# Products with the values alternated between a pair's two heads, the output projection's first chunk amid the pairs, and rows 128 to 255 turned in score banks

## The chip, the core and the metric

The kernel runs on one core of a Trainium2 chip. TensorE (PE in the rows; PEld is its weight load) multiplies, VectorE (DVE) and ScalarE (ACT) do the elementwise work and empty PSUM, GpSimd (POOL) and SyncE (SP) issue most of the transfers. PSUM has eight banks of 128 partitions by 512 float32 values here. The metric is the device time of one execution in microseconds (us), the median of several. Less is better.

## What is computed

Two residual layers over 512 tokens of width 1024. Layer 0 mixes tokens by causal pooling, layer 1 by dilated sliding-window attention; after each mixer comes a SwiGLU feed-forward with 2816 hidden units, and a last rmsnorm ends it. The change touches only layer 1's mixer:

```python
def attn_mixer(h, w_qkv, w_out):
    qkv = jnp.einsum('bsd,de->bse', h, w_qkv).reshape(B, S, 3, N_HEADS, HEAD_DIM)
    q = rope(qkv[:, :, 0]) * HEAD_DIM ** -0.5
    k, v = rope(qkv[:, :, 1]), qkv[:, :, 2]
    ...
    for (window, dilation), n_g in zip(((128, 1), (512, 4), (2048, 16)), (6, 5, 5)):
        o_g, lse_g = dilated_window_attention(q[:, :, sl], k[:, :, sl], v[:, :, sl], window, dilation)
    ...
    merged = concat of the groups, each times 3 * alpha (a softmax over the groups' lse)
    return jnp.einsum('bse,ed->bsd', merged, w_out)
```

There are 16 heads of width 64. Heads 0 to 5 (the near heads) see windows of 128 tokens: a block of 128 queries meets its own block of keys and the one before. Heads 6 to 15 (the far heads) see every fourth or sixteenth token: with the tokens sorted by residue modulo 4, a block of 128 queries meets one block of keys.

## The kernel before, in words

**Precision.** Most products are three: an operand x is kept as a rounded part `hi` and the rest `lo`, and `hi·hi + hi·lo + lo·hi` is summed in a PSUM bank (`mm3`; lines 403 to 405 in the output projection). ScalarE makes `hi` by a cast (L171 for weights, L361 for activations) and VectorE makes `lo` by a subtraction (L175, L362). The scores (L1020, L1051) and the products with the values (L1290 to L1294) are plain float32 products: each leaves two records on PE, called passes below.

**Turning the rows (L1104 to L1120).** The attention works on feature-major activations `h`. After layer 0's feed-forward, rows 0 to 255 of the residual are normalised last. `late(b)` calls `turned`, which makes eight 128x128 transposes of row block b into two PSUM tiles, four into each, and then splits each tile into `h_hi` and `h_lo` by a cast (L361) and a subtraction (L362). Both `late(0)` and `late(1)` take their two tiles from the pool `ptr` (tiles `tp`), which has two banks. They stand inside `by_halves`, which makes the first three of the q and k projections, the products of tokens 256 to 511 first (they do not need rows 0 to 255): `late(0)` stands in the middle of the second projection's products, `late(1)` ahead of the third's. Another pool, `psc` (tiles `sc`), also has two banks; its first use is the scores of the first pair of heads, some 18 us later.

**Products with the values (L1281 to L1303).** For each pair t of heads (2t, 2t+1) one PSUM tile `mm` of 128 partitions takes the result: the even head writes partitions 0 to 63, the odd head 64 to 127. The loop goes over the heads, and within a head over four blocks b of 128 queries. A far head has one product a block (L1290), a near head one with its own block (L1292) and, for b over 0, one with the block before (L1294): a near pair has 14 products (28 passes), a far pair 8 (16 passes), all eight pairs 82 (164 passes). Then VectorE multiplies the tile by the heads' weights, spread over the partitions (`o`, L1298 for t below 3, L1302 else), ScalarE casts `o` into `m_hi`, and VectorE subtracts into `m_lo`. Those share the buffers of `h`. The weights come by transfers that POOL issues (`weights_of`, L1214) into three ring tiles `LB` and two halves of `even_rows`; the ring is used again for pairs 5, 6 and 7. The pool `mm` has four banks, so pair t waits until VectorE has read pair t-4's tile.

**Output projection (`out_projection`, from L393).** Its first half of columns goes in four chunks i, each with two of the eight pairs (contraction blocks 2i and 2i+1) and one weight tile, over four row blocks b, into four banks held open (two `sc`, two `tp`): 24 products of 512 columns a chunk. It has a `hook`, called after chunk 0, which attention does not use. The second half of the columns follows row block by row block, and with it the residual's sum, the norm and the turn for layer 1's feed-forward.

**What sets the order.** TensorE's order is the order of the code (`manual_schedule` for PE). A scheduler orders VectorE and ScalarE. Two weight casts of the next feed-forward are tied behind the last pair's split (`cast_behind`, `behind`).

Of the kernel before, what the change touches and what calls it, by code (L numbers as in the profile page):

```python
# [10 lines left out]
F32 = mybir.dt.float32  # L11
# [6 lines left out]
P = 128  # L18
S = 512
D = 1024  # L20
NC = D // P
# [3 lines left out]
HD = 64  # L25
# [13 lines left out]
SHIFT = 32  # L39
# [36 lines left out]
def trunk_kernel(ctx: ExitStack, tc: tile.TileContext, x_in, xT, gam, gains, consts, ident_d, w0, wT, w1, wv, w_down, out):  # L76
# [9 lines left out]
    nc = tc.nc  # L86
# [27 lines left out]
    queue = []  # L114
# [145 lines left out]
    j_wo = [wo(2 * i, 0) for i in range(4)] + [wo(2 * i, 1, pool="b") for i in range(4)]  # L260
# [23 lines left out]
    def tokens_at(shift):  # L284
        both = tokens_both(shift)
        return [both[:, z] for z in range(2)]
# [73 lines left out]
    def split(hi, lo, src, eng=None):  # L360
        cast = nc.scalar.copy(hi, src)  # L361
        return cast, (eng or nc.vector).tensor_sub(lo, src, hi.bitcast(F32))  # L362

    def in_order(b):

        return lambda h, half, tp: (h[:, 4 * half : 4 * half + 4, b * P : (b + 1) * P], tp)

    def by_residue(b):

        n = P // R  # L370

        def places(h, half, tp):
            at = h[:, 4 * half : 4 * half + 4, :].rearrange("p c (r j) -> p c r j", r=R)
            return at[:, :, :, b * n : (b + 1) * n], tp.rearrange("p c (i r) -> p c r i", r=R)

        return places

    def turned(norm, shift, b, tps, order):

        hi, lo = tokens_at(shift)  # L380
        for half, tp in enumerate(tps):
            norm.turn(b, half, tp)
        for half, tp in enumerate(tps):
            (to_hi, src), (to_lo, _) = order(hi, half, tp), order(lo, half, tp)
            with tc.high_priority(URGENT):
                split(to_hi, to_lo, src)

    def into_stream(b, half, ps, quarter=None):
        cs = COLS[half] if quarter is None else QUARTERS[quarter]
        with tc.high_priority(URGENT):  # L390
            nc.vector.tensor_add(x[:, b, cs], ps, x[:, b, cs])

    def out_projection(js, where, hi, lo, norm, shift, four, tps, hook=None):  # L393

        def products(ps, w, at, b):
            for k in range(2):
                c = where[at + k]
                cols = slice(b * P, (b + 1) * P)  # L400
                xhi, xlo = hi[:, c, cols], lo[:, c, cols]
                first, last = at + k == 0, at + k == NC - 1
                nc.tensor.matmul(ps, lhsT=xhi, rhs=w[0][:, k, :], start=first, stop=False)  # L403
                nc.tensor.matmul(ps, lhsT=xhi, rhs=w[1][:, k, :], start=False, stop=False)  # L404
                nc.tensor.matmul(ps, lhsT=xlo, rhs=w[0][:, k, :], start=False, stop=last)  # L405

        for i in range(4):
            w = weights(js[i])
            for b in range(4):
                products(four[b], w, 2 * i, b)  # L410
                if i == 3:
                    into_stream(b, 0, four[b])
                    norm.square(b, 0)
            if i == 0 and hook:
                hook()
        ws = [weights(js[4 + i], split_ahead=4 + i, load_ahead=6 + i) for i in range(4)]
        for b in range(4):
            norm.gained(b, 0)
            ps = mm.tile([P, S], F32, name="mm")
            for i in range(4):  # L420
                products(ps, ws[i], 2 * i, b)
            if b in (1, 2):
                turned(norm, shift, b - 1, tps(), in_order(b - 1))
            into_stream(b, 1, ps)
            norm.square(b, 1)
            norm.gained(b, 1)
            if b < 3:
                norm.prepare(b)
        tps = [mm.tile([P, S], F32, name="mm").rearrange("p (j t) -> p j t", j=4) for _ in range(2)]
        for half in range(2):  # L430
            norm.turn(2, half, tps[half])
        return tps
# [5 lines left out]
    with ExitStack() as pctx:  # L438
# [26 lines left out]
        for c in range(NC):  # L465
# [17 lines left out]
            for b, i in turns:  # L483
# [3 lines left out]
                    start=c == 0 and i == 0, stop=c == NC - 1 and i == 2, skip_group_check=True,  # L487
# [3 lines left out]
        norm = Norm(None, spare)  # L491
# [11 lines left out]
        v, s, r = (tmp.tile([P, 4], F32, name=name) for name in ("v4", "s4", "r4"))  # L503
# [66 lines left out]
        norm = Norm(0, px.tile([P, D], F32, name="even_rows"))  # L570
# [6 lines left out]
        third = out_projection(j_out, BY_GROUP, z_hi, z_lo, norm, SHIFT, [mm.tile([P, S], F32, name="mm") for _ in range(4)], turned_banks, lambda: group_products(1, early))  # L577
# [376 lines left out]
    norm = ffn(0, norm, third, 1)  # L954


    with ExitStack() as actx:
# [4 lines left out]
        psc = actx.enter_context(tc.tile_pool(name="psc", bufs=2, space=bass.MemoryType.PSUM))  # L962
        ptr = actx.enter_context(tc.tile_pool(name="ptr", bufs=2, space=bass.MemoryType.PSUM))

        at = 8 * SPAN
# [3 lines left out]
        pT = ap.tile([P, 6 * 7 + 10 * 4, P], F32, name="pT")  # L969
        v = ap.tile([P, 4, D], F32, name="v")  # L970
# [28 lines left out]
        def slot(h, i):  # L999
            return h * 7 + i if h < 6 else 42 + (h - 6) * 4 + i  # L1000
# [100 lines left out]
                pend_tr.extend((step + 2 + n // 2, *got) for n, got in enumerate(run(*args)))  # L1101

        h_hi, h_lo = tokens_at(0)
        late = lambda b: turned(norm, 0, b, [ptr.tile([P, 4, P], F32, name="tp") for _ in range(2)], by_residue(b))  # L1104

        def by_halves(js):

            n = J // 2
            part = lambda z, i: z.rearrange("p (r j) -> p r j", r=R)[:, :, i * n : (i + 1) * n]
            got = [(mm.tile([P, S], F32, name="mm"), weights(j, held=i)) for i, j in enumerate(js)]  # L1110
            for i in (1, 0):
                for at, (ps, (whi, wlo)) in enumerate(got):
                    if i == 1 and at == 2:
                        late(1)
                    for c in range(NC):
                        if (i, at, c) == (1, 1, NC // 2):
                            late(0)
                        mm3(part(ps, i), whi[:, c, :], wlo[:, c, :], part(h_hi[:, c, :], i), part(h_lo[:, c, :], i),
                            i == 1 and c == 0, c == NC - 1, skip_group_check=True)
            return [ps for ps, _ in got]  # L1120
# [120 lines left out]
        for m in range(3):  # L1241
            ps = project(j_v0[m], h_hi, h_lo)
# [7 lines left out]
        for part in range(2):  # L1250
            at = VA + part * VB
            pv = [mm.tile([P, S], F32, name="mm") for _ in range(4)]
            for c in range(4):
                whi, wlo = weights(j_v[part][c])
                for b in range(4):
                    for kk in range(2):
                        kc = 2 * c + kk
                        o = pv[b][:, :VB]
# [19 lines left out]
        two = mp.tile([P, D], F32, name="even_rows")  # L1278
        of_heads = [weights_of(t, to) for t, to in enumerate(ring + [two[:, cs] for cs in COLS])]
        m_hi, m_lo = h_hi, h_lo  # L1280
        for t in range(8):  # L1281
            ps = mm.tile([P, S], F32, name="mm")
            for h in (2 * t, 2 * t + 1):
                base = HD * (h % 2)
                rows = slice(base, base + HD)
                cols = slice(h * HD, (h + 1) * HD)
                for b in range(4):
                    o = ps[rows, b * P : (b + 1) * P]
                    if h >= 6:
                        nc.tensor.matmul(o, lhsT=v[:, b, cols], rhs=pT[:, slot(h, b), :], start=True, stop=True)  # L1290
                    else:
                        nc.tensor.matmul(o, lhsT=v[:, b, cols], rhs=pT[:, slot(h, 2 * b), :], start=True, stop=b == 0)  # L1292
                        if b:
                            nc.tensor.matmul(o, lhsT=v[:, b - 1, cols], rhs=pT[:, slot(h, 2 * b - 1), :], start=False, stop=True)  # L1294
            o = mp.tile([P, S], F32, name="o", bufs=2)
            with tc.high_priority(URGENT):
                if t < 3:
                    nc.vector.tensor_mul(o, ps, of_heads.pop(0))  # L1298
                    of_heads.append(weights_of(5 + t, ring[t]))
                else:  # L1300
                    by_r = lambda z: z.rearrange("p (r j) -> p r j", r=R)
                    nc.vector.tensor_mul(o.rearrange("p (j r) -> p r j", r=R), by_r(ps), by_r(of_heads.pop(0)))  # L1302
                last = split(m_hi[:, t, :], m_lo[:, t, :], o)  # L1303
        for j in (j_wo[-1] + 1, j_wo[-1] + 2):
            queue[j].update(cast_behind=last[0].ins, behind=last[1].ins)
        norm = Norm(2, mp.tile([P, D], F32, name="even_rows"))
        sc_tile = lambda: psc.tile([P, 4, P], F32, name="sc")
        four = [sc_tile(), sc_tile()] + [ptr.tile([P, 4, P], F32, name="tp") for _ in range(2)]
        four = [t.rearrange("p r j -> p (r j)") for t in four]
        third = out_projection(j_wo, range(NC), m_hi, m_lo, norm, SHIFT, four, lambda: [sc_tile(), sc_tile()])  # L1310

    ffn(1, norm, third, 3)
    mm.close()
# [67 lines left out]
```

## Time and profile before

| | us |
|---|---|
| median of 3 runs | 989.33 |
| lowest, highest | 989.17, 989.90 |
| the profiled execution | 989.87 |
| its span | 988.1 |
| PE busy | 979.4 (99%) |
| VectorE busy | 786.5 (80%) |
| ScalarE busy | 573.2 (58%) |

The profile is of one execution; 1.8 us of its time lie outside the span. Times in rows count from the span's start. The stages that matter here: the q and k projections begin at 440.6, the products with the values run from 599.05 to 611.40, the output projection from there to some 657, and layer 1's feed-forward from there to the end. Consecutive matmuls overlap in the records, so what a product costs is the distance from its start to the next one's, not its own duration.

### The profile page before, as it was taken

Reading aid. Unit: us, or ns where it says so; the run is one execution under the profiler, and the core shown is the slowest. Engines: PE = TensorE matmul, PEld = TensorE weight load, DVE = VectorE, ACT = ScalarE, POOL = GpSimd, SP = SyncE. Lnnn points to the kernel's source line nnn. Section 1 sums busy time; section 2 is a strip of 40 time slices with the busy share of each in tenths; the row PEclk is TensorE's granted clock in tenths of the full one; section 3 lists DMA queues with packets and bytes.
Section 4 is the critical chain, followed back from the end, with each engine's and each line's share of the span. In section 5 each row is a group of like instructions: output and inputs, shape, how many; then the busy total and the mean of one; then the engine's idle time right before and its main releaser. Section 6 shows DMA issues by size and latency. Waiting matters only on the chain.

```text
span 988.1 us, 15369 instructions
## 1 busy us (share of the span) xinstructions
PE 979.4 (99%) x5914; PEld 870.5 (88%) x5914; DVE 786.5 (80%) x1088; ACT 573.2 (58%) x898; POOL 124.6 (13%) x124
## 2 busy tenths in 40 slices
PE   9999999999999999999999999999999999999997
PEld 8888899989988999888888899899998898899886
DVE  6475799898988888787887547579989798888876
ACT  6573666646765666573442544357664676567655
POOL 0001010010011111101121123100101001110110
PEclk9999999999999999999999999999999999999999
DMA  9448277479569867554221249526847946987652
GB/s 341 176 161 201 43 199 177 127 197 254 145 153 243 232 169 164 127 196 150 73 69 54 62 139 280 117 55 172 206 120 209 255 128 161 245 223 193 145 135 103
DMA packets 79465, 162.98 MB, mean 165 GB/s; under 512 B 6096, under 2 KB 6480, under 8 KB 79392
## 3 DMA queue, kind: packets, MB, share of 16 engines
q1 hardware_dynamic: 58544, 122.04, 37.6%
q0 software_dynamic: 20560, 39.69, 23.4%
q8 instruction: 46, 0.75, 0.3%
q10 hardware_dynamic: 288, 0.27, 0.1%
q14 instruction: 27, 0.22, 0.1%
HBM read 159.85 MB, written 2.13 MB: 164 GB/s over the span
## 4 chain that ended last, share of the span: by engine, by line
PE 96%; DVE 2%; ACT 2%; issue 0%; ACTq 0%
PE pair L674 32%; PE pair L818 20%; PE p L700 5%; PE mm L264 4%; PE mm L266 4%; PE mm L265 4%; PE pair L700 4%; PE r L700 2%; PE early L485 2%; PE mm L405 2%; PE mm L403 2%; PE mm L404 2%; PE mm L700 1%; PE tp L1081 1%; PE mm L1260 1%; PE mm L1261 1%
## 5 line engine op out<-in xcount | busy, mean ns | idle before, releaser
L175 DVE TENSOR_TENSOR wlo<-wraw,whi 128x1024 fp32r<-128x1024 f32 (+2 forms) x190 | 220.4, 1165 | 66.7 <-ACT whi L171 66.1
L171 ACT CAST whi<-wraw 128x1024 fp32r<-128x1024 f32 (+2 forms) x189 | 183.9, 979 | 148.1 <-issue 32.1
L171 ACT CAST whi<-vraw 128x1024 fp32r<-128x1024 f32 (+1 forms) x108 | 105.2, 980 | 118.3 <-DVE vraw L177 39.4
L175 DVE TENSOR_TENSOR wlo<-vraw,whi 128x1024 fp32r<-128x1024 f32 (+1 forms) x108 | 121.6, 1133 | 46.2 <-ACT whi L171 46.2
L674 PE MATMUL pair<-h,whi 128*128 128x512 f32 (+1 forms) x640 | 143.2, 349 | 0.0
L674 PEld LDWEIGHTS pair<-h,whi 128*128 128x128 f32 x640 | 109.1, 189 | 13.4
L674 PE MATMUL pair<-t,whi 128*128 128x512 f32 (+1 forms) x512 | 110.6, 337 | 0.0
L818 PE MATMUL pair<-whi,u_hi 128*128 128x512 f32 (+1 forms) x284 | 109.9, 387 | 0.0
L818 PE MATMUL pair<-wlo,u_hi 128*128 128x512 f32 (+1 forms) x284 | 109.9, 387 | 0.0
L818 PE MATMUL pair<-whi,u_lo 128*128 128x512 f32 (+1 forms) x284 | 109.7, 386 | 0.0
L674 PEld LDWEIGHTS pair<-t,whi 128*128 128x128 f32 x512 | 86.0, 190 | 8.4
L674 PE MATMUL pair<-h,wlo 128*128 128x256 f32 x512 | 89.2, 281 | 0.0
L674 PEld LDWEIGHTS pair<-h,wlo 128*128 128x128 f32 x512 | 76.1, 188 | 4.2
L138 POOL DMA_DIRECT2D wraw<-w x22 | 26.6, 1211 | 395.6 <-DMA wraw<-w 131.6
L177 DVE TENSOR_TENSOR vraw<-vraw,wraw 128x1024 f32<-128x1024 f32 (+1 forms) x66 | 75.2, 1140 | 0.7
L674 PE MATMUL pair<-t,wlo 128*128 128x256 f32 x384 | 71.9, 282 | 0.0
L264 PE MATMUL mm<-h,whi 128*128 128x512 f32 (+1 forms) x176 | 64.9, 368 | 0.0
L266 PE MATMUL mm<-h,wlo 128*128 128x512 f32 (+1 forms) x176 | 63.6, 361 | 0.0
L265 PE MATMUL mm<-h,whi 128*128 128x512 f32 (+1 forms) x176 | 63.4, 360 | 0.0
L818 PEld LDWEIGHTS pair<-whi,u_lo 128*128 128x128 f32 x284 | 53.3, 188 | 10.8
L818 PEld LDWEIGHTS pair<-whi,u_hi 128*128 128x128 f32 x284 | 53.4, 188 | 10.4
L818 PEld LDWEIGHTS pair<-wlo,u_hi 128*128 128x128 f32 x284 | 53.4, 188 | 10.2
(346 smaller groups left out, 2044.8 us busy)
## 6 DMA issues: line engine op xcount, KB each, us to landing
wraw<-w SPq DMA_DIRECT2D x116, 512.0 KB, 4.7
wraw<-w_down SPq DMA_DIRECT2D x32, 512.0 KB, 4.1
vraw<-w SPq DMA_DIRECT2D x22, 512.0 KB, 4.7
wraw<-w POOLq DMA_DIRECT2D x22, 512.0 KB, 7.7
vraw<-w POOLq DMA_DIRECT2D x22, 512.0 KB, 8.7
wraw<-wT SPq DMA_DIRECT2D x16, 512.0 KB, 4.4
vraw<-w_down POOLq DMA_DIRECT2D x12, 512.0 KB, 7.5
wraw<-w_down SPq DMA_DIRECT2D x24, 256.0 KB, 3.2
```

The source lines that it names most:

```text
L138: nc.gpsimd.dma_start(dst, more, accum_op=ALU.add)
L171: nc.scalar.copy(hi[:, :n], raw[:, :n])
L175: nc.vector.tensor_sub(lo[:, :n], raw[:, :n], hi[:, :n].bitcast(F32))
L177: nc.vector.tensor_add(raws[into][:, :n], raws[into][:, :n], raws[more][:, :n])
L264: nc.tensor.matmul(ps, lhsT=whi, rhs=xhi, start=first, stop=False, **kw)
L265: nc.tensor.matmul(ps, lhsT=whi, rhs=xlo, start=False, stop=False, **kw)
L266: nc.tensor.matmul(ps, lhsT=wlo, rhs=xhi, start=False, stop=last, **kw)
L403: nc.tensor.matmul(ps, lhsT=xhi, rhs=w[0][:, k, :], start=first, stop=False)
L404: nc.tensor.matmul(ps, lhsT=xhi, rhs=w[1][:, k, :], start=False, stop=False)
L674: mat = lambda o, w, m, **kw: nc.tensor.matmul(o, lhsT=w, rhs=m, skip_group_check=True, **kw)
L700: nc.tensor.matmul(ps[:, g, :], lhsT=w[:, g, c, :], rhs=right[:, z, c, :], start=i in (0, 1, 3) and g + c + k == 0, stop=c == 3 and k == 2 ...
L818: nc.tensor.matmul(acc(t), lhsT=u, rhs=w, start=first, stop=n == len(places) - 1, skip_group_check=True)
```

## The change

Three edits. (1) `late(1)` takes its two PSUM tiles from `psc` instead of `ptr`. (2) The loop over a pair's products goes over the blocks first and alternates between the two heads; the set of products is the same. (3) Pairs 0 to 5 come first, then chunk 0 of the output projection (it needs pairs 0 and 1), then, as its hook, pairs 6 and 7, then chunks 1 to 3.

```diff
-        late = lambda b: turned(norm, 0, b, [ptr.tile([P, 4, P], F32, name="tp") for _ in range(2)], by_residue(b))
+        late = lambda b, pool, name: turned(norm, 0, b, [pool.tile([P, 4, P], F32, name=name) for _ in range(2)], by_residue(b))
...
-                        late(1)
+                        late(1, psc, "sc")
...
-                            late(0)
+                            late(0, ptr, "tp")
...
-        for t in range(8):
+        def merged(t):
             ps = mm.tile([P, S], F32, name="mm")
-            for h in (2 * t, 2 * t + 1):
-                base = HD * (h % 2)
-                rows = slice(base, base + HD)
-                cols = slice(h * HD, (h + 1) * HD)
-                for b in range(4):
-                    o = ps[rows, b * P : (b + 1) * P]
-                    if h >= 6:
-                        nc.tensor.matmul(o, lhsT=v[:, b, cols], rhs=pT[:, slot(h, b), :], start=True, stop=True)
-                    else:
-                        nc.tensor.matmul(o, lhsT=v[:, b, cols], rhs=pT[:, slot(h, 2 * b), :], start=True, stop=b == 0)
-                        if b:
+            for b in range(4):
+                for own in (True, False):
+                    for h in (2 * t, 2 * t + 1):
+                        base = HD * (h % 2)
+                        o = ps[base : base + HD, b * P : (b + 1) * P]
+                        cols = slice(h * HD, (h + 1) * HD)
+                        if own:
+                            at = slot(h, b) if h >= 6 else slot(h, 2 * b)
+                            nc.tensor.matmul(o, lhsT=v[:, b, cols], rhs=pT[:, at, :], start=True, stop=h >= 6 or b == 0)
+                        elif h < 6 and b:
                             nc.tensor.matmul(o, lhsT=v[:, b - 1, cols], rhs=pT[:, slot(h, 2 * b - 1), :], start=False, stop=True)
...
-                last = split(m_hi[:, t, :], m_lo[:, t, :], o)
-        for j in (j_wo[-1] + 1, j_wo[-1] + 2):
-            queue[j].update(cast_behind=last[0].ins, behind=last[1].ins)
+                return split(m_hi[:, t, :], m_lo[:, t, :], o)
+
+        def last_merged():
+            for t in (6, 7):
+                cast, rest = merged(t)
+            for j in (j_wo[-1] + 1, j_wo[-1] + 2):
+                queue[j].update(cast_behind=cast.ins, behind=rest.ins)
+
+        for t in range(6):
+            merged(t)
...
-        third = out_projection(j_wo, range(NC), m_hi, m_lo, norm, SHIFT, four, lambda: [sc_tile(), sc_tile()])
+        third = out_projection(j_wo, range(NC), m_hi, m_lo, norm, SHIFT, four, lambda: [sc_tile(), sc_tile()], last_merged)
```

TensorE's queue at the turn of rows 128 to 255, ahead of the third projection's first product, in the kernel before (`tp` is a tile of `ptr`):

```order
L358 MATMUL tp_4308<-ident_84,odd_rows_81 128x128 x4
L358 MATMUL tp_4309<-ident_84,odd_rows_81 128x128 x4
L264 MATMUL mm_4245<-h_74,whi_4232 128x4x64
L265 MATMUL mm_4245<-h_74,whi_4232 128x4x64
...
```

and in the changed one (`sc` is a tile of `psc`):

```order
L358 MATMUL sc_4308<-ident_84,odd_rows_81 128x128 x4
L358 MATMUL sc_4309<-ident_84,odd_rows_81 128x128 x4
L264 MATMUL mm_4245<-h_74,whi_4232 128x4x64
L265 MATMUL mm_4245<-h_74,whi_4232 128x4x64
...
```

The place is the same; only the tiles written are others. TensorE's queue where the pairs begin, in the kernel before (`mm_5590` is the last bank of the v projection, `mm_5739` pair 0's tile, `mm_5760` pair 1's; one head's seven products are the first six rows after the v projection's):

```order
L1262 MATMUL mm_5590<-whi_5593,h_74 128x320
L1292 MATMUL mm_5739<-pT_4215,v_4216 64x128 x2
L1294 MATMUL mm_5739<-pT_4215,v_4216 64x128
L1292 MATMUL mm_5739<-pT_4215,v_4216 64x128
L1294 MATMUL mm_5739<-pT_4215,v_4216 64x128
L1292 MATMUL mm_5739<-pT_4215,v_4216 64x128
L1294 MATMUL mm_5739<-pT_4215,v_4216 64x128
L1292 MATMUL mm_5739<-pT_4215,v_4216 64x128 x2
```

and in the changed one:

```order
L1262 MATMUL mm_5590<-whi_5593,h_74 128x320
L1292 MATMUL mm_5739<-pT_4215,v_4216 64x128 x4
L1294 MATMUL mm_5739<-pT_4215,v_4216 64x128 x2
L1292 MATMUL mm_5739<-pT_4215,v_4216 64x128 x2
L1294 MATMUL mm_5739<-pT_4215,v_4216 64x128 x2
L1292 MATMUL mm_5739<-pT_4215,v_4216 64x128 x2
L1294 MATMUL mm_5739<-pT_4215,v_4216 64x128 x2
L1292 MATMUL mm_5760<-pT_4215,v_4216 64x128 x4
```

Each x2 is now one product of the even head and one of the odd head, and the 14 products of a pair stand in four blocks instead of two runs of seven. TensorE's queue from the far pairs to the output projection, in the kernel before (`mm_5802` to `mm_5854` are pairs 3 to 7, `whi_5629` is chunk 0's weight, `whi_5659` chunk 1's):

```order
L1290 MATMUL mm_5802<-pT_4215,v_4216 64x128 x8
L1290 MATMUL mm_5815<-pT_4215,v_4216 64x128 x8
L1290 MATMUL mm_5828<-pT_4215,v_4216 64x128 x8
L1290 MATMUL mm_5841<-pT_4215,v_4216 64x128 x8
L1290 MATMUL mm_5854<-pT_4215,v_4216 64x128 x8
L403 MATMUL sc_5871<-whi_5629,h_74 128x512
...
L405 MATMUL tp_5874<-whi_5629,h_74 128x512
L403 MATMUL sc_5871<-whi_5659,h_74 128x512
```

and in the changed one (pairs 3 to 5 are `mm_5802` to `mm_5828`, pairs 6 and 7 `mm_5879` and `mm_5892`):

```order
L1292 MATMUL mm_5802<-pT_4215,v_4216 64x128 x8
L1292 MATMUL mm_5815<-pT_4215,v_4216 64x128 x8
L1292 MATMUL mm_5828<-pT_4215,v_4216 64x128 x8
L403 MATMUL sc_5845<-whi_5629,h_74 128x512
...
L405 MATMUL tp_5848<-whi_5629,h_74 128x512
L1292 MATMUL mm_5879<-pT_4215,v_4216 64x128 x8
L1292 MATMUL mm_5892<-pT_4215,v_4216 64x128 x8
L403 MATMUL sc_5845<-whi_5659,h_74 128x512
```

Chunk 0's 24 products moved ahead of pairs 6 and 7; a far pair's eight products now alternate between the heads too. On VectorE, ScalarE, POOL and SP every instruction keeps its place.

## Rows read from the trace of the kernel before

**Rows 1.** The page, part 4: the chain that ended last, shares by engine.
```profile
PE 96%; DVE 2%; ACT 2%; issue 0%; ACTq 0%
```

**Rows 2.** TensorE's waits in the whole span: us in total, times, longest.
```profile
...
PE tp L358 <- DVE h L362: 0.9, 1, 0.9
PE mm L1260 <- ACT ropea L1246: 0.3, 1, 0.3
```

**Rows 3.** Timeline of all engines, 444.8 to 449.4: start, duration, instruction, count, idle before.
```profile
444.80 0.28 PE L266 MATMUL mm<-h,wlo 128*128 128x256 f32 x1
...
445.32 2.34 DVE L175 TENSOR_TENSOR wlo<-wraw,whi 128x1024 fp32r<-128x1024 f32 x2
445.44 1.34 ACT L352 ACTIVATE odd_rows<-odd_rows,r 128x512 f32<-128x512 f32 x2 [0.74 <-DVE r L343]
445.71 0.36 PE L264 MATMUL mm<-h,whi 128*128 128x256 f32 x1
...
447.10 0.28 PE L266 MATMUL mm<-h,wlo 128*128 128x256 f32 x1
447.58 1.28 DVE L362 TENSOR_TENSOR h<-tp,h 128x512 fp32r<-128x512 f32 x2
448.32 1.25 PE L358 MATMUL tp<-ident,odd_rows 128*128 128x128 f32 x8 [0.94 <-DVE h L362]
...
449.33 0.36 PE L264 MATMUL mm<-h,whi 128*128 128x256 f32 x1
```

**Rows 4.** Timeline of TensorE where the near pairs begin, 598.6 to 601.4.
```profile
598.67 0.31 PE L1261 MATMUL mm<-wlo,h 128*128 128x320 f32 x1
598.82 0.31 PE L1262 MATMUL mm<-whi,h 128*128 128x320 f32 x1
599.05 0.65 PE L1292 MATMUL mm<-pT,v 128*64 128x128 f32 x4
...
599.98 0.38 PE L1294 MATMUL mm<-pT,v 128*64 128x128 f32 x2
600.20 0.44 PE L1292 MATMUL mm<-pT,v 128*64 128x128 f32 x4
600.41 0.27 PE L1294 MATMUL mm<-pT,v 128*64 128x128 f32 x1
...
601.35 0.44 PE L1292 MATMUL mm<-pT,v 128*64 128x128 f32 x4
```

**Rows 5.** Timeline of TensorE, the far pairs and the output projection's begin.
```profile
606.33 5.15 PE L1290 MATMUL mm<-pT,v 128*64 128x128 f32 x77
611.40 0.50 PE L403 MATMUL sc<-whi,h 128*128 128x512 f32 x1
611.74 0.39 PE L404 MATMUL sc<-wlo,h 128*128 128x512 f32 x1
611.97 0.39 PE L405 MATMUL sc<-whi,h 128*128 128x512 f32 x1
```

**Rows 6.** Timeline of TensorE, a far pair's scores, which alternate between row halves.
```profile
534.73 1.06 PE L1051 MATMUL mm<-k,q 64*128 64x128 f32 x16
535.72 0.50 PE L264 MATMUL mm<-h,whi 128*128 128x512 f32 x1
```

**Rows 7.** Timeline of VectorE: the weighting of pairs 0, 1 and 7.
```profile
601.98 0.69 DVE L1298 TENSOR_TENSOR o<-mm,LB 128x512 f32<-128x512 f32 x1 [0.80 <-PE mm L1294]
...
604.28 0.69 DVE L1298 TENSOR_TENSOR o<-mm,LB 128x512 f32<-128x512 f32 x1 [0.23 <-PE mm L1294]
...
615.07 1.07 DVE L1302 TENSOR_TENSOR o<-mm,LB 128x512 f32<-128x512 f32 x1 [0.68 <-DMA LB<-far]
```

**Rows 8.** Busy time by stretch: length, PE, PEld, DVE, ACT, POOL, clock, DMA share.
```profile
645.00:658.00 13.00, 13.00 (x70) 10.98 (x68) 7.65 (x20) 6.08 (x13) 0.00 (x0) 1.00 0.17 29
658.00:680.00 22.00, 22.00 (x188) 22.00 (x187) 21.94 (x31) 15.88 (x27) 0.00 (x0) 1.00 0.42 130
680.00:720.00 40.00, 40.00 (x330) 39.65 (x329) 38.60 (x49) 27.14 (x35) 5.76 (x5) 1.00 0.74 187
```

## The prediction, made before the changed kernel ran

> **What bounds the kernel now.** I read the chain that ended last first: 96% of the span is TensorE, and what waits for nothing is 0% [rows 1]. So the time changes by what TensorE's own queue gains or loses, and work taken from another engine is worth nothing unless TensorE waits for it. Then TensorE's waits: two in the region of the change, 0.9 us for VectorE ahead of a turn and 0.3 us for ScalarE elsewhere [rows 2]. The rest is TensorE's own pace, and the third view is therefore the timeline of its queue, read from start to start, since the records overlap.
>
> **Edit 1, rows 128 to 255 turned in score banks.** A turn with free banks is `late(0)`: the last product ahead of it starts at 444.80, the first behind it at 445.71, 0.91 us apart. Around `late(1)` the same distance is 447.10 to 449.33, 2.23 us [rows 3]. The eight transposes are equal, so 1.32 us are waits: 0.94 ahead of the first transpose, the rest ahead of the second tile. The releaser is VectorE's L362, which empties the two `tp` banks of `late(0)` from 447.58 to 448.86, behind two weight subtractions (445.32 to 447.66). Score banks have no such reader. What is next late: the rows themselves, which ScalarE has scaled by 445.44 + 1.34 = 446.78, 0.4 us ahead of TensorE's arrival at 447.2. Behind the turn stand 24 products that do not need it; 445.71 to 447.10 shows 12 of them in 1.4 us, so they cover some 2.9 us, and VectorE's four subtractions (two at 0.64 each from 447.58, two more behind them) end by about 450.2, while TensorE would want rows 0 to 255 at 450.9. Gain 1.3 us; bounds 0.9 (the first wait alone) and 1.3.
>
> **Edit 2, alternating the heads.** All pairs take 599.05 to 611.40, 12.35 us for 164 passes. Inside one head two passes stand from 599.98 to 600.20, 0.11 us each. Where the odd head's run begins, the rows of the two heads mix: the four passes that start at 600.20 last 0.44 in all, so their starts lie (0.44 - 0.27) / 3 = 0.057 us apart, and at 600.41 the other head's L1294 stands among them [rows 4]. So the two halves of the columns do run beside each other, each at its 0.11 us, but only over a few passes at the change of heads. A near head therefore takes 600.20 to 601.35, 1.15 us for 14 passes, 0.082 each; the far pairs, with runs of 8, take (5.15 - 0.27) / 76 = 0.064 each [rows 4, 5].
>
> With the heads alternating, a slot of 0.110 us should hold one pass of each: 82 slots, 9.02 us. A form that alternates throughout exists in this trace, with row halves in place of column halves: 16 passes of a far pair's scores span 1.06 us, so eight slots start (1.06 - 0.27) / 7 = 0.113 us apart [rows 6]. That makes 9.3 us at the worst such slot and 8.94 at 0.109. What stays of the ends: the first passes spread over 0.65 in place of 0.27 + 3 x 0.11 = 0.60 (0.05 us), and the last pass, which starts at 606.33 + 5.15 - 0.27 = 611.21, is 0.19 ahead of the next product instead of 0.11 (0.08 us) [rows 4, 5]. So 12.35 becomes 9.02 + 0.13 = 9.15, a gain of 3.2 us. The lower bound for a pairing that works only as well as in the far pairs now, 0.064 a pass, is 164 x 0.064 = 10.5 us, a gain of 1.7.
>
> **Edit 3, chunk 0 ahead of pairs 6 and 7.** TensorE now enters and leaves the 64-column form twice. The price of one more entry and exit, from the rows: the first value product stands 0.23 behind the last projection's where 0.15 is the step (0.08), the 0.05 above, the 0.08 above, and the second product of the output projection stands 0.34 behind the first where 0.23 is the step (0.11) [rows 4, 5]. Sum 0.32 us, a loss. No product is added. Who waits for the move? Pair t needs the bank of pair t-4. By the slots TensorE would start pair 4 at about 604.6 and pair 5 at 605.4; VectorE read pairs 0 and 1 by 602.67 and 604.97 already in the slower order [rows 7], and gets them earlier now. Chunk 0 would start at 606.3, and its first three products need only pair 0; pair 1's weighting ends at 604.97 now, and a cast and a subtraction of the same size (0.69 each at most) end by 606.4 even at today's times. Queued behind pair 7's split on ScalarE and VectorE are only the two weight casts of the feed-forward, wanted some 40 us later. Pair 7's weighting stands at 615.07 now and waits 0.68 us for its weights' transfer [rows 7]; in the new order TensorE finishes pair 7 at about 614, so this stands where it was; chunk 3, which needs it, starts two chunks of 24 x 0.23 = 5.5 us later, at 625. Cost of the move: 0.32 us, nothing else.
>
> **Sum.** 1.32 + 3.20 - 0.32 = 4.2 us, if what lies behind moves along. It should: from 645 to 658 VectorE is busy 7.65 of 13 us and the transfers take 0.17 of their engines [rows 8], so there both have caught up and wait for TensorE, and the feed-forward behind starts from the same state, only earlier. The profiled execution (989.87, span 988.1, 1.8 us outside) lies 0.54 over the median of 989.33. Span 983.9, profiled execution 985.7, median 989.33 - 4.2 = **985.1**.
>
> **The rivals.**
> (A) *No pairing.* Both heads' products use all 128 rows; if a weight load of one half could not start beside the other half's running product, alternation would leave 12.35 us as they are. Left are edit 1's gain and edit 3's loss: 989.33 - 1.32 + 0.32 = 988.3. Against it stand the mixed records at 600.20 to 600.58 [rows 4]. The Trainium skill states such a rule in "TensorE: Matmul & The Clock Gate", Part 3 (packing small matmuls): weight loads overlap products in flight only where the row groups differ. By it the time would be 988.3; this trace does not agree, with 0.057 us between starts of products that all use 128 rows.
> (B) *The feed-forward's VectorE becomes the bound.* It is busy 21.94 of 22 and 38.60 of 40 us from 658 to 720 [rows 8]. If its work could not start earlier, TensorE could gain only what VectorE idles there, 0.06 + 1.40 = 1.5 us: 987.9. Against it: the idle time just ahead of 658, on PE's account.
> (C) *Slower: two halves of one bank exclude each other.* Where the trace shows column halves together, they write different columns of a bank, or different banks; in the new order they write the same columns of one bank, on other partitions, at once. If that serialised, each pass would stand alone at 0.11: 164 x 0.11 = 18.0 us in place of 12.35, hence 989.33 + 5.7 - 1.3 + 0.3 = 994.0. It decides from (12.35 + 1.32 - 0.32) / 164 = 0.081 us a pass on. No row shows this case; the row halves of rows 6 write two banks. The Trainium skill, "PSUM — Partial Sum Buffer", section on bank collisions, quotes a guide by which different column tiles may access one bank at once on disjoint partitions; by it the sum stays 985.1, and I give (C) a small chance.
> (D) *Only edit 1 fails*, because the turn waits for something else (the scaled rows come later): 989.33 - 2.88 = 986.4.
>
> **How the numbers follow.** Forecast 0.76, (A) 0.07, (B) 0.06, (C) 0.05, (D) 0.06. The forecast's own range: upwards, 0.9 for edit 1 and 1.7 for edit 2 with the 0.32 lost leave 2.3 us, 987.0; downwards 1.32 + 3.41 - 0.2 = 4.5, 984.8, and another 0.5 for the distance between executions (989.17 to 989.90): 984.3. That range to 987.2 takes in (D) and most of the forecast, and leaves out (A), (B) and (C), 0.18. A measurement of this kernel tells about 0.2%, 2 us, from no change: faster means below 987.35, slower above 991.3. The forecast and (D) are faster, 0.82; (A) and (B) within, 0.13; (C) slower, 0.05.
>
> **What would show it.** Edit 1: the distance across the turn into `sc` falls from 2.23 to 0.9 us, and VectorE's wait row vanishes from TensorE's list. Edit 2: pairs 0 to 5 (132 passes) take about 7.3 us to chunk 0's first product; records of the same line stand 0.055 us apart throughout. If they stand 0.08 or more apart, pairing failed. Edit 3: about 0.3 us more at chunk 0's two edges. Behind it: everything from 660 on should stand 4.2 us earlier, with no new wait of TensorE; waits for VectorE or ScalarE between 690 and 760 would mean (B). I would be wrong above all if the two heads' runs of two passes do not overlap as the ends of long runs do.

## The result

| us | before | after |
|---|---|---|
| median | 989.43 (989.03 to 989.90, 6 runs) | 985.44 (984.98 to 986.30, 6 runs) |
| the profiled execution | 989.87 | 986.30 |
| its span | 988.1 | 984.5 |

The ratio is 0.996, with a 95% interval from 0.9948 to 0.9973: faster by 4.0 us, where 4.2 were forecast. The forecast of 985.1 and its range hold.

The changed kernel's waits of TensorE over the whole span (us in total, times, longest):

```profile
PE mm L302 <- DVE odd_rows L296: 1.1, 1, 1.1
PE mm L1260 <- ACT ropea L1246: 0.3, 1, 0.3
PE early L485 <- DVE h L461: 0.2, 1, 0.2
```

The wait for L362 ahead of the turn [rows 2] is no longer there, and none has come in its place between the turn and the feed-forward; the third row, which the kernel before does not have, stands at 12.86 us, at the start of the program. TensorE's timeline at the two turns of the changed kernel (start, duration, instruction, count):

```profile
445.43 0.28 PE L266 MATMUL mm<-h,wlo 128*128 128x256 f32 x1
445.55 1.04 PE L358 MATMUL tp<-ident,wraw 128*128 128x128 f32 x8
446.34 0.36 PE L264 MATMUL mm<-h,whi 128*128 128x256 f32 x1
...
447.73 0.28 PE L266 MATMUL mm<-h,wlo 128*128 128x256 f32 x1
447.85 1.03 PE L358 MATMUL sc<-ident,odd_rows 128*128 128x128 f32 x8
448.64 0.36 PE L264 MATMUL mm<-h,whi 128*128 128x256 f32 x1
```

From the product ahead of a turn to the one behind it now pass 0.91 us for either turn; the second took 2.23 [rows 3]. The first line of this fence also starts later than its counterpart: 445.43 against 444.80, so this execution was 0.63 us behind before it reached the change.

TensorE's timeline from the first pair to chunk 2 of the output projection, in the changed kernel:

```profile
598.32 0.66 PE L1292 MATMUL mm<-pT,v 128*64 128x128 f32 x8
...
599.90 0.61 PE L1292 MATMUL mm<-pT,v 128*64 128x128 f32 x8
...
601.43 0.61 PE L1292 MATMUL mm<-pT,v 128*64 128x128 f32 x8
...
602.96 2.79 PE L1292 MATMUL mm<-pT,v 128*64 128x128 f32 x48
605.68 0.50 PE L403 MATMUL sc<-whi,h 128*128 128x512 f32 x1
...
611.36 1.97 PE L1292 MATMUL mm<-pT,v 128*64 128x128 f32 x32
613.26 0.50 PE L403 MATMUL sc<-whi,h 128*128 128x512 f32 x1
...
618.83 0.39 PE L403 MATMUL sc<-whi,h 128*128 128x512 f32 x1
```

and in the kernel before, where the pairs began at 599.05 [rows 4], the first products of chunks 1 and 2:

```profile
616.98 0.39 PE L403 MATMUL sc<-whi,h 128*128 128x512 f32 x1
...
622.42 0.39 PE L403 MATMUL sc<-whi,h 128*128 128x512 f32 x1
```

The runs of mixed lengths [rows 4] have become even ones: a near pair takes 601.43 - 599.90 = 1.53 us, the 48 passes of pairs 3 to 5 stand (2.79 - 0.27) / 47 = 0.054 apart on the mean, and pairs 0 to 5 take 598.32 to 605.68, 7.36. By the single starts in the trace the passes come in couples: 0.007 us apart within a couple, and the next couple 0.102 behind. From here on I measure each kernel by the distance from its first pair product to chunk 2's first product, since every edge of the 64-column form then lies inside: 23.37 us before, 20.51 after, 2.86 less.

Behind it the time stays: TensorE's last product starts at 977.81, 358.98 behind chunk 2's first, and in the kernel before 981.39 - 622.42 = 358.97. Busy time by stretch, in the columns of rows 8 and 4 us earlier:

```profile
654.00:676.00 22.00, 22.00 (x189) 22.00 (x187) 21.94 (x31) 15.68 (x26) 0.00 (x0) 1.00 0.38 128
676.00:716.00 40.00, 40.00 (x330) 39.65 (x329) 38.60 (x50) 27.23 (x36) 5.77 (x5) 1.00 0.73 187
```

VectorE is as full as before (21.94 and 38.60), with about as many instructions (31 and 50): what it does there starts earlier.

### The profile page after: what moved, and what is told of

It is laid out like the page before. It is cut to its first block, busy times and chain, and to the rows that moved or that the text cites. A ratio compares the mean times of both kernels' runs of the same rounds, so it can differ in the third digit from the quotient of the medians.

```text
span 984.5 us, 15370 instructions
## 1 busy us (share of the span) xinstructions
PE 976.3 (99%) x5914; PEld 866.6 (88%) x5914; DVE 786.1 (80%) x1088; ACT 573.0 (58%) x898; POOL 124.6 (13%) x124
## 4 chain that ended last, share of the span: by engine, by line
PE 97%; ACT 1%; DMA 1%; DVE 1%; SPq 0%; issue 0%; DVEq 0%; ACTq 0%
PE pair L674 32%; PE pair L818 21%; PE p L700 5%; PE mm L264 4%; PE mm L266 4%; PE mm L265 4%; PE pair L700 4%; PE r L700 2%; PE mm L405 2%; PE mm L403 2%; PE mm L404 2%; PE early L485 2%; PE mm L700 1%; PE tp L1081 1%; PE mm L1260 1%; PE mm L1261 1%
## 5 line engine op out<-in xcount | busy, mean ns | idle before, releaser
L175 DVE TENSOR_TENSOR wlo<-wraw,whi 128x1024 fp32r<-128x1024 f32 (+2 forms) x190 | 220.3, 1164 | 64.5 <-ACT whi L171 63.9
L175 DVE TENSOR_TENSOR wlo<-vraw,whi 128x1024 fp32r<-128x1024 f32 (+1 forms) x108 | 121.5, 1133 | 46.5 <-ACT whi L171 46.5
```

The costliest lines, as they stand in the source:

```text
L175: nc.vector.tensor_sub(lo[:, :n], raw[:, :n], hi[:, :n].bitcast(F32))
```

## The experiments

All distances are read from TensorE's timeline as above; the expectations on record speak of the distance to chunk 1's first product, so the table has both.

| | median us (runs) | to chunk 1 | to chunk 2 |
|---|---|---|---|
| before | 989.43 (6) | 17.93 | 23.37 |
| after | 985.44 (6) | 14.94 | 20.51 |
| edit 1 alone | 988.27 (11) | 17.93 | 23.37 |
| edits 1, 2 | 985.16 (5) | 15.56 | 21.00 |
| edit 3 alone | 990.43 (10) | 18.55 | 24.12 |
| alternating within one half | 991.90 (10) | 21.57 | 27.15 |
| runs of three | 985.70 (5) | 15.50 | 21.09 |
| one more switch | 985.64 (5) | 15.31 | 20.88 |
| edits 1, 2, rests one later | 984.84 (5) | 14.70 | 20.14 |
| after, second profile | 985.13 (5) | 14.93 | 20.50 |
| edits 1, 2, second profile | 985.16 (5) | 14.69 | 20.13 |

The kernel before had 989.49 beside the first four experiments of the table, 989.57 beside the next two and 989.2 beside the last three; the ratios below are to these.

**Edit 1 alone.** The kernel before with only the turn's tiles moved:

```diff
-                        late(1)
+                        late(1, psc, "sc")
```

> The kernel before with edit 1 alone: rows 128 to 255 are turned in the score pool's banks. Theory 1 (the wait for the two transpose banks is all that edit 1 removes, and what lies behind moves along): across that turn TensorE goes from 2.23 us to 0.91, everything behind stands 1.3 us earlier to the end, 988.1 us. Rival (the gain is given back at the next wait, the 0.3 us for ScalarE near 571, or in the feed-forward behind, where VectorE is busy 98%): 1.3 us earlier behind the turn, but less than 0.7 at the end, 988.8 or more.

Measured: 988.27, ratio 0.9987 (0.9978 to 0.9996), 1.2 us less than the kernel before beside it. Its turn on TensorE's timeline:

```profile
446.77 0.28 PE L266 MATMUL mm<-h,wlo 128*128 128x256 f32 x1
446.89 1.03 PE L358 MATMUL sc<-ident,odd_rows 128*128 128x128 f32 x8
447.68 0.36 PE L264 MATMUL mm<-h,whi 128*128 128x256 f32 x1
```

0.91 us: the whole 1.32 is edit 1's. It stays, since the distances behind are those of before: from the first product behind the turn to the first pair 149.70 us, 149.72 before, and then the table's. So the rival on record, that the gain is given back behind, falls, and with it the prediction's (D), that the rows are what is late.

**Edit 3 alone.** The order of the products inside a pair as before; chunk 0 ahead of pairs 6 and 7:

```diff
+        for t in range(6):
+            merged(t)
-        third = out_projection(j_wo, range(NC), m_hi, m_lo, norm, SHIFT, four, lambda: [sc_tile(), sc_tile()])
+        third = out_projection(j_wo, range(NC), m_hi, m_lo, norm, SHIFT, four, lambda: [sc_tile(), sc_tile()], last_merged)
```

> The kernel before with edit 3 alone: heads one after the other as before, chunk 0 between pairs 5 and 6. Theory 1: one more entry and exit (0.32 us), and in addition the few passes that ran side by side across the border of pairs 5 and 6 now stand alone: 3.5 slots of 0.109, 0.38 us. From the first pair's first product to chunk 1's first product 17.9 us become 18.6, and the time is 0.7 us above the kernel before, 990.1. Rival (only the form's switch costs): 18.2 us, 989.75. Rival (the order frees VectorE, which is late there): not slower than before.

Measured: 990.43, ratio 1.0006 (0.9997 to 1.0015); the interval takes in no change, so the trace has to speak. The first products of the first pair, of chunk 1 and of chunk 2 on the timeline:

```profile
598.91 0.65 PE L1293 MATMUL mm<-pT,v 128*64 128x128 f32 x4
...
617.46 0.50 PE L403 MATMUL sc<-whi,h 128*128 128x512 f32 x1
...
623.03 0.39 PE L403 MATMUL sc<-whi,h 128*128 128x512 f32 x1
```

18.55 us to chunk 1 against an expected 18.6, and 0.75 more than before to chunk 2. By itself the move costs.

**Alternating within one half.** As the changed kernel, but TensorE alternates between the even heads of two pairs, then between their odd heads. Two products that stand next to each other then use different banks but the same columns of the array:

```diff
+            for i in range(2):
+                lists = [product_list(t + n, banks[n], 2 * (t + n) + i) for n in range(2)]
+                for at in range(max(map(len, lists))):
+                    for todo in lists:
+                        make(todo[at : at + 1])
```

> The changed kernel, but products alternate between the even heads of two pairs (both in columns 0 to 63, two banks), then between their odd heads. Theory 1 (what runs side by side are the two column halves, and only where both stand among the next few passes): runs of 28, 22, 16 and 16 passes in one half pair only over about 3.5 slots at each change of half, some 140 slots of 0.109, 15.3 us for all products with the values instead of 9; the time is 6 us above the changed kernel, about 991.7, more than before the change. Rival (any alternation between two banks and two weights hides the latency of a product, whichever half): 9 us as in the changed kernel, 985.4.

Measured: 991.90, ratio 1.0024 (1.0015 to 1.0033). Its value products on the timeline:

```profile
597.33 12.72 PE L1295 MATMUL mm<-pT,v 128*64 128x128 f32 x132
609.98 0.50 PE L403 MATMUL sc<-whi,h 128*128 128x512 f32 x1
...
615.65 3.33 PE L1295 MATMUL mm<-pT,v 128*64 128x128 f32 x32
618.90 0.50 PE L403 MATMUL sc<-whi,h 128*128 128x512 f32 x1
```

The passes of pairs 6 and 7 stand (3.33 - 0.27) / 31 = 0.099 us apart on the mean, with one change of half among them, and 0.109 apart within a half; the changed kernel's stand (1.97 - 0.27) / 31 = 0.055 apart. So it is the other half of the columns that makes a pass cheap, not the change of head, of bank or of accumulation. (The other half of the columns also writes the other 64 partitions; the two go together in every run here.) My 15.3 us for all value products was too low (12.65 + 3.25 = 15.90). In the kernel before, 164 x 0.110 = 18.04 us are shortened to 12.35 at 15 changes of half, 0.38 each; this run has six such changes, five among pairs 0 to 5 and one in pairs 6 and 7, hence 18.04 - 6 x 0.38 = 15.8. The 3.5 slots a change were right (3.5 x 0.109 = 0.38), the count was not: six changes leave 164 - 21 = 143 slots, 15.6 us, not some 140, and the ends of the two stretches, which I left out, make the rest.

**Runs of three.** As the changed kernel, but three products of the even head, then three of the odd head:

```diff
+        RUN = 3
+            for at in range(0, len(lists[0]), RUN):
+                for todo in lists:
+                    make(todo[at : at + RUN])
```

> The changed kernel, but the heads alternate after three products (six passes) instead of one: runs of 6, 6 and 2 passes in a near pair, 6 and 2 in a far one. Theory 1, with the size of the look-ahead from the kernel before (a run of 14 passes takes 10.5 slots of 0.109, a run of 8 takes 4.5: 3.5 slots are saved a run, whatever its length): a run of six needs no more than its three slots, so the products with the values take the same 9.0 us as in the changed kernel (within 0.3), 985.4. Rival (only the product next to a change of head runs side by side, two passes a run): runs of 6 take 4 slots, some 104 slots instead of 82, 2.4 us more, 987.8.

Measured: 985.70, ratio 0.9964 (0.9949 to 0.9979): within the noise of the changed kernel, and far from the rival's 987.8. The trace is finer:

```profile
597.14 7.69 PE L1295 MATMUL mm<-pT,v 128*64 128x128 f32 x132
604.76 0.50 PE L403 MATMUL sc<-whi,h 128*128 128x512 f32 x1
...
610.47 2.24 PE L1295 MATMUL mm<-pT,v 128*64 128x128 f32 x32
612.64 0.50 PE L403 MATMUL sc<-whi,h 128*128 128x512 f32 x1
```

7.62 + 2.17 = 9.79 us for all value products, against 7.36 + 1.90 = 9.26 in the changed kernel. Both stretches lose about the same 0.27, whether they hold 132 passes or 32. So a run of six passes is paired as fully as a run of two; only where a stretch starts or ends does one half stand alone for longer (the first two and the last two steps take 0.109 us or more, those between 0.055 on the mean). The expected 9.0, within 0.3, left those ends out and missed; the rival's 2.4 us more falls.

**One more switch.** As the changed kernel, but pair 6 stands in the middle of chunk 0 and pair 7 behind it, so that TensorE goes into the 64-column form three times instead of two:

```diff
+                if i == 0 and amid and b % 2:
+                    amid(6 + b // 2)
```

> The changed kernel with chunk 0 in two halves: two row blocks, pair 6, two row blocks, pair 7. The same products and one more entry and exit of the 64-column form. Theory 1 (a switch pair costs 0.32 us wherever it stands): from the first pair's first product to chunk 1's first product 14.94 us become 15.26, 985.75. Rival (the 0.32 us were the cost of leaving chunk 0's weights or banks, not of the form): no change. Rival (each switch waits for what is under way, half a product of 512 columns more): 15.5 or more.

Measured: 985.64, ratio 0.9962 (0.9947 to 0.9976), and 15.31 us to chunk 1 against an expected 15.26; to chunk 2 20.88, 0.37 over the changed kernel.

```profile
607.61 1.09 PE L1294 MATMUL mm<-pT,v 128*64 128x128 f32 x16
608.63 0.50 PE L403 MATMUL tp<-whi,h 128*128 128x512 f32 x1
...
611.57 1.09 PE L1294 MATMUL mm<-pT,v 128*64 128x128 f32 x16
612.60 0.50 PE L403 MATMUL sc<-whi,h 128*128 128x512 f32 x1
```

A pair of 16 passes takes 1.02 to 1.03 us from its first product to the next full-width one, where 8 slots of 0.109 are 0.87: the entries and exits have a price of their own, and it adds up per switch.

**Edits 1 and 2, chunk 0 where it was.** All eight pairs first, then the output projection:

```diff
+        for t in range(8):
+            cast, rest = merged(t)
```

> The changed kernel without edit 3: all eight pairs, heads alternating, then chunks 0 to 3. Theory 1 (edit 3 costs one more entry and exit of the 64-column form, 0.32 us, and hides nothing): pairs 6 and 7 find their banks read (VectorE read pair 2 by 605.31 and pair 3 by 606.32 in the changed kernel's trace, TensorE would come at 605.6 and 606.5), so from the first pair's first product to chunk 1's first product 14.94 us become 14.62, and the time is 0.3 us below the changed kernel, 985.1. Rival (edit 3 hides VectorE: without chunk 0 ahead of them, pairs 6 and 7 wait for the banks of pairs 2 and 3): TensorE shows waits of some 1 us there, 15.6 us for the same distance, 986 or more.

Measured: 985.16, ratio 0.9958 (0.9945 to 0.9970). The time is the theory's, but the profiled execution (985.85) is the rival's: 15.56 us to chunk 1, and a wait. TensorE, VectorE and ScalarE there, three timelines:

```profile
597.41 0.66 PE L1292 MATMUL mm<-pT,v 128*64 128x128 f32 x8
...
602.05 2.79 PE L1292 MATMUL mm<-pT,v 128*64 128x128 f32 x48
605.28 2.16 PE L1292 MATMUL mm<-pT,v 128*64 128x128 f32 x32 [0.44 <-DVE o L1298]
```

```profile
599.45 1.23 DVE L175 TENSOR_TENSOR blo<-wraw,bhi 128x1024 fp32r<-128x1024 f32 x1 [1.44 <-ACT bhi L171]
600.59 0.68 DVE L1298 TENSOR_TENSOR o<-mm,LB 128x512 f32<-128x512 f32 x1
601.96 0.69 DVE L362 TENSOR_TENSOR h<-o,h 128x512 fp32r<-128x512 f32 x1 [0.69 <-ACT h L361]
...
603.94 0.69 DVE L362 TENSOR_TENSOR h<-o,h 128x512 fp32r<-128x512 f32 x1 [0.69 <-ACT h L361]
604.55 0.68 DVE L1298 TENSOR_TENSOR o<-mm,LB 128x512 f32<-128x512 f32 x1
605.15 1.15 DVE L1302 TENSOR_TENSOR o<-mm,even_rows 128x512 f32<-128x512 f32 x1
```

```profile
598.37 1.05 ACT L171 CAST bhi<-wraw 128x1024 fp32r<-128x1024 f32 x1 [2.18 <-DMA wraw<-wT]
```

Pair 6 needs the bank of pair 2, and pair 2's weighting (the L1298 at 604.55) ends at 605.23; TensorE starts pair 6 at 605.28. Pair 7 is held too, by pair 3's bank: its weighting (L1302) ends at 606.30, and pair 7 starts at 606.35, 0.25 us behind pair 6's last pass instead of 0.10; no wait row shows that, since the records overlap. With the slower passes at each restart the two stops cost 0.87 us against the second profile of this kernel, below. Read backwards: pair 2's weighting stands behind two subtractions, ahead of each of which VectorE idles 0.69 us for ScalarE's cast of `o`; the first weighting stands behind a weight's subtraction (L175), this behind that weight's cast, and the cast waited 2.18 us for its transfer. Two further runs look at both links.

**Edits 1 and 2, rests one pair later.** The same order on TensorE; VectorE weights pair t + 1 before it subtracts pair t's rest:

```diff
+        def rest_of(t, o, mul):
+            with tc.high_priority(URGENT), tc.issue_after(mul.ins):
+                return nc.vector.tensor_sub(m_lo[:, t, :], o, m_hi[:, t, :].bitcast(F32))
...
+            o, mul, cast = merged(t)
+            if t:
+                rest_of(t - 1, before, mul)
```

> Edits 1 and 2 without 3 (as in the run with the chunk not moved), and VectorE subtracts pair t's rest behind pair t+1's weighting instead of ahead of it; TensorE's order is that of the run with the chunk not moved. In that run 15.56 us went from the first pair's first product to chunk 1's first, and TensorE waited 0.4 us ahead of pair 6 for VectorE's weighting of pair 2 (same bank), which began at 604.55 although pair 2's products were done by 602.3. Theory: it stood behind two subtractions, for each of which VectorE idled 0.69 us until ScalarE's cast. With the new order pair 2 is weighted by about 603.3, the wait is gone, the distance is 14.57 to 14.62 us, and the time lies about 0.9 us under that of the chunk not moved and 0.3 under the changed kernel, some 984.3 to 985.1. Rival: VectorE's eight weightings with their subtractions are too much work for the faster pairs whatever their order; then the wait moves to another pair and the distance stays at 15.3 or more.

**The changed kernel, and edits 1 and 2, beside it.**

> The changed kernel once more, as the measure for the two other runs beside it on the same chip: 14.94 us from the first pair's first product to chunk 1's first, 985.4 us.

> Edits 1 and 2 without 3 once more. Its first trace showed 15.56 us from the first pair's first product to chunk 1's first, 0.62 more than the changed kernel, though its median was no longer. If the trace is right and the medians differed by what lies outside this stretch, the time is 0.5 to 0.6 us above the changed kernel's in this call. Rival: something behind the stretch gives the 0.6 back; then the two times are within 0.2 of each other, and the products behind stand nearer than 0.6.

Measured, on one chip: 984.84 (984.51 to 985.45) with the rests later, 985.13 (984.83 to 985.43) for the changed kernel, 985.16 (984.79 to 985.44) for edits 1 and 2; ratios 0.9954, 0.9955 and 0.9956. Nothing tells the three medians apart. My expectation of 0.5 to 0.6 us more for edits 1 and 2 failed, and that of 0.9 less for the rests placed later with it. The rival's number held (within 0.2), but not its reason: nothing behind gave time back, the wait itself was absent from the profiled execution of edits 1 and 2. Its TensorE, VectorE and ScalarE:

```profile
597.31 0.66 PE L1292 MATMUL mm<-pT,v 128*64 128x128 f32 x8
...
601.94 4.54 PE L1292 MATMUL mm<-pT,v 128*64 128x128 f32 x80
...
617.44 0.39 PE L403 MATMUL sc<-whi,h 128*128 128x512 f32 x1
```

```profile
598.30 1.23 DVE L175 TENSOR_TENSOR blo<-wraw,bhi 128x1024 fp32r<-128x1024 f32 x1 [0.40 <-ACT bhi L171]
...
603.41 0.68 DVE L1298 TENSOR_TENSOR o<-mm,LB 128x512 f32<-128x512 f32 x1
```

```profile
597.22 1.04 ACT L171 CAST bhi<-wraw 128x1024 fp32r<-128x1024 f32 x1 [1.14 <-DMA wraw<-wT]
```

The transfer came early enough for the cast to start at 597.22 instead of 598.37, everything on VectorE follows 1.15 us earlier, pair 2's weighting ends at 604.09, and TensorE wants the bank at 601.94 + 48 x 0.0546 = 604.56. So the slack was 0.47 us for pair 6 here (0.31 for pair 7, by the same sum) and below zero in the first profile: by the chain read above, the same code waits or not by when one weight lands. It is the transfer's own time that differs, not its issue: SyncE issued it 7.05 us ahead of the first pair in the first profile and 7.06 in the second (590.36 and 590.25), and it took 8.0 us until the cast could start in the first and 7.0 in the second. No run moved that transfer by itself; why it is late, and how often, is open.

With the rests later, VectorE gets to pair 2 earlier. TensorE, VectorE and ScalarE in that run:

```profile
596.91 0.66 PE L1292 MATMUL mm<-pT,v 128*64 128x128 f32 x8
...
601.55 4.54 PE L1292 MATMUL mm<-pT,v 128*64 128x128 f32 x80
```

```profile
600.85 0.68 DVE L1307 TENSOR_TENSOR h<-o,h 128x512 fp32r<-128x512 f32 x1
601.77 0.69 DVE L1298 TENSOR_TENSOR o<-mm,LB 128x512 f32<-128x512 f32 x1 [0.24 <-PE mm L1294]
```

```profile
596.31 1.05 ACT L171 CAST bhi<-wraw 128x1024 fp32r<-128x1024 f32 x1 [0.62 <-DMA wraw<-wT]
```

VectorE now waits for TensorE instead of ScalarE, and pair 2 is weighted by 602.46, 1.7 us ahead of TensorE's need (its 80 passes began at 601.55, so pair 6 at 604.2). The distance is 20.14 us, the same as without the reordering in the undisturbed profile. In this execution the weight came early too (its cast began 0.60 us ahead of the first pair), so that this order would also stand a late weight is an argument from the slack, not shown.

## Why the prediction was right, step by step

**Edit 1.** Predicted 1.32, measured 1.32 (2.23 to 0.91), in the changed kernel and with the edit alone. The upper bound was the right one because it was read from the distance between full products. Its split was misread: by starts the first transpose came 1.10 us late, not 0.94 (448.32 - 447.10 = 1.22 [rows 3], against 0.12 in the free turn; the wait row counts idle time alone), and 0.22 came behind it, 0.11 of that ahead of the second tile and the rest in the two slower restarts.

**Edit 2.** Predicted 3.20. Without the chunk's move and without a wait it is 23.37 - 20.13 = 3.24, by the second profile of edits 1 and 2. The slot of 0.110 us for one pass of each head was the term that had to hold: 132 passes took 7.36 us against a forecast of about 7.3. Rival (A), no pairing, falls with it. The Trainium skill's rule in "TensorE: Matmul & The Clock Gate", Part 3, is that weight loads overlap products in flight only where row groups differ; the 0.055 us between products that all use 128 rows does not agree with it. Rival (C) falls as well: column halves that write the same columns of one bank run beside each other, at the same 0.055 us a pass. The Trainium skill, "PSUM — Partial Sum Buffer", quotes in its section on bank collisions a guide by which different column tiles may access one bank at once on disjoint partitions; the trace agrees.

**Edit 3.** Predicted +0.32, "nothing else". The price of one more entry and exit is 20.51 - 20.13 = 0.38 by the undisturbed profiles, 0.37 by the extra switch, 0.05 to 0.06 over the sum of edges. Edit 3 alone costs 0.75: that price and one change of half less, 0.38. What the step overlooked is that pairs 6 and 7 are the tightest users of a bank: I asked only about pairs 4 and 5 in the new order, and not who would wait in the old order once the pairs are fast. With edits 1 and 2 alone the wait cost 21.00 - 20.13 = 0.87 us in one of two profiles; chunk 0 between pair 5 and pair 6 gives those banks 5.7 us more, and neither profile of the changed kernel shows the wait. So edit 3 pays 0.38 in every execution to avoid 0.87 in some; whether that is worth it is open, since the medians with and without it are the same (985.13 and 985.16 side by side). The sum was not touched, because it was made for all three edits together.

**What lies behind.** Predicted to move along, and so it did: 358.97 and 358.98 us from chunk 2 to the last product. Rival (B) falls: VectorE's work in that stretch did start earlier, and its full share held nothing back.

**The sum.** 1.32 + 2.86 = 4.18 by the traces, 4.2 forecast; that it is so near is in part luck, since edit 2 gave 0.04 more than its term and edit 3 cost 0.06 more than its own. The profiled execution shows 3.6, because it came 0.63 us later to the turn than the profiled execution of before: its 51st matmul already starts at 13.90 us instead of 13.28; its second profile (985.43) and the medians have no such loss. That start lies between 12.47 and 13.90 in the eleven profiles, ahead of everything that the runs change, so single executions differ by up to 1.4 us before they reach the change.

## What to carry to other kernels

Where products use only half of the array's columns, look at the distance between starts where the halves change: if it halves there, alternate the halves throughout, in runs as short as the code allows but not necessarily of one. Before a stretch of TensorE's queue is made faster, count for each buffer that it takes again how long its reader has left; what was free by microseconds may now hang on one late transfer. A median that fits the theory is no proof of its mechanism: here one kernel had the forecast time with the rival's trace, and the next profile of the same code had neither the wait nor another time.

## What the runs showed of the hardware

- Two column halves run beside each other at 0.055 us a pass, against 0.109 where neighbours use the same half, even if these write different banks.
- The pairing does not need strict alternation: runs of six passes a half are paired as fully as runs of two, with 0.27 us lost at the two ends of each stretch together.
- Going from 128-column products to 64-column ones and back costs 0.37 to 0.38 us in both places where a switch was added.
- In two executions of the same code one weight's transfer, issued at the same distance ahead of the first pair product, released its cast 0.96 us behind that product in one (598.37 against 597.41) and 0.09 ahead of it in the other (597.22 against 597.31).
